# Putting off the second half of the softmax, giving the fourth output block and two rows of x a buffer of their own, and loading the branch rows two at a time, in a two-layer diffusion step

## The chip, the cores and the metric

One program runs on one core of a Trainium2 chip. The metric is the device time of one execution in microseconds (us). A core has five engines with an instruction stream each, executed in order: PE (TensorE, matrix products into PSUM), DVE (VectorE), ACT (ScalarE), POOL (GpSimd) and SP (SyncE, which here only issues transfers). They wait for one another through semaphores. Transfers run on 16 DMA engines that all issuers share.

## The reference, cut to what matters

Two layers work on 1280 tokens of 1024 channels: 256 context tokens (`x_prompt`) and 1024 latent tokens (`x_sample`). Layer 0 mixes tokens with a gated linear scan (GLA, 4 heads, forwards and backwards), layer 1 with softmax attention (8 heads of 128, 2 key heads; a latent query sees 1024 latent and 256 cached keys, a context query 256 context keys). Each layer normalises and modulates its input, projects it, mixes, multiplies by a SiLU gate, projects with `w_out`, and adds the result times a per-channel gate `gt` to `x`.

```
hs = rms_norm(xs, norm_g[l]) * (1.0 + sc_s) + sh_s
y  = (mixer(hs @ w_in) * silu(gate)) @ w_out
xs = xs + gt_s * y
p  = softmax(q @ keys.T * scale);  o = p @ vals        # layer 1
```

The outputs are both streams after layer 1, the scan states, and the new keys and values.

## The kernel before

Every matrix operand is held as two float16 parts, hi and lo, and every product is three matmuls (hi·hi, hi·lo, lo·hi) that accumulate in float32. So a row or a weight block must be scaled, split into hi and lo, and, where it is the contracted side, transposed by a DMA before PE can use it. Tokens come in tiles of 128 rows; tiles 0 and 1 are context, 2 to 9 latent. The transposed, modulated activations of all tokens stay on chip in `hT_hi` and `hT_lo`. Weight blocks live in three kept places (`wtile(0)`, `wtile(1)`, `wtile(2)`), each with a hi and a lo half of 512 columns; `wst` is a small ring of staging buffers, `wada` another one for the modulation weights.

The program runs in stages. A list scheduler in the language orders each engine's instructions from the order in which the code issues them; `issue_after(x)` gives code the place right behind instruction x.

- **Load and modulation, then the GLA loop** (`gla`, from about 140 us). Five passes h over ten tiles n; slot = 10h + n. In each slot a tile's scan and gate work is interleaved with fillers from the function `filler(slot)`: modulation weights, weights of layer 1 split ahead of time, and from slot 32 the output projection of layer 0. At the slots in `WO` (32, 36, 38, 40) a quarter of `w_out` (256 columns) is staged, and `fill_out` scales and splits it (DVE L161, L175; ACT L174): the first two into place 0, the third into the place that the last gate block used, the fourth into place 2. At slot 43 `fold_gate` loads the gate row `gt_d` and multiplies it by the four blocks' inverse scales on POOL (L712, eight instructions). At the slots in `PREP` (42, 44, 46) a finished branch row `og_d[i]` (128 tokens, 512 KB) is loaded, measured (DVE L745), split (ACT L748, DVE L749) and transposed (SP L751, L752); at those in `EARLY` (45, 47) tiles 2 and 3 get their `residual` (output projection, times gate, plus x) and are stored to `x1_d`.
- **gla_out** (about 582 to 782 us). For the ten tiles in the order 2 to 9, 0, 1: `residual` (PE L125 into the banks y; DVE L723 times gate, L724 plus x), and per pair of tiles `normalise` (ACT L329, DVE L332), PE transposes (L337) and `modulate` (ACT L348, POOL L349, DVE L350), then `key_tile`, which projects keys and values, normalises and rotates the keys and transposes them. Tiles 2 and 3 are read back from `x1_d`. `out_load` loads the next branch row into `og`, which has one buffer; `out_prep` is as above, with one DMA transpose of 2048 columns into `ogT` (SP L754).
- **attention** (about 782 to 1258 us). Ten steps (a half of the heads, a block of 256 queries) of four heads e. `scores(h, c, j, ...)` does one softmax tile of 128 queries by 1280 keys: nine matmuls into S (PE L974), the row maximum (DVE L977), its scaling (ACT L979), the exponential p with its row sum (ACT L982), the reciprocal (DVE L984, L986), the hi part of p divided (POOL L989), the lo part (DVE L990) and one DMA transpose into PT (SP L991). S has two buffers in PSUM, p and the pair phl two, PT three, one for each head. `values` (30 matmuls with PT, then DVE L1015) is two heads behind; `query`/`query_rest` (24 matmuls of 512 columns and the work on ACT, DVE and POOL) prepare the queries of a later step; two `gateT` (24 matmuls each) stand at the end of every second head.
- **att_out** (from about 1258 us): the output projection of layer 1, row by row, stored to the output.

For a pair of heads (plain and with a prime) the code before writes S0, query, S1, V, S0', S1', V', G, G; on PE the scheduler puts the first 11 of the 30 matmuls of V' ahead of S1'.

## Time and profile before

| | |
|---|---|
| median of three runs | 1352.31 us (1348.84 to 1357.2) |
| the profiled execution | 1360.72 us |
| its span in the trace | 1358.9 us |
| mean granted PE clock | 0.978 |
| PE busy | 1245.7 us, 92% |
| DVE, ACT, POOL busy | 69%, 49%, 28% |
| moved by DMA | 199.14 MB, mean 147 GB/s |

The profile is of one execution, somewhat slower than the median. A busy time of PE of 92% is a mean over stages: the idle time sits in particular places, and the waits table of a window says how often and for how long an engine stood idle, and which instruction of which engine ended the wait. A wait is written "waiter <- releaser". The windows table gives for each stretch the length, then busy us of each engine, the granted PE clock, the share of time that the DMA engines were busy, and GB/s.

### The profile page before, as it was taken

Reading aid. Unit: us, or ns where it says so; the run is one execution under the profiler, and the core shown is the slowest. Engines: PE = TensorE matmul, PEld = TensorE weight load, DVE = VectorE, ACT = ScalarE, POOL = GpSimd, SP = SyncE. Lnnn points to the kernel's source line nnn. Section 1 sums busy time; section 2 is a strip of 40 time slices with the busy share of each in tenths; the row PEclk is TensorE's granted clock in tenths of the full one; section 3 lists DMA queues with packets and bytes.
Section 4 is the critical chain, followed back from the end, with each engine's and each line's share of the span. In section 5 each row is a group of like instructions: output and inputs, shape, how many; then the busy total and the mean of one; then the engine's idle time right before and its main releaser. Section 6 shows DMA issues by size and latency. Waiting matters only on the chain. (4 is left out here: it accounts for less than half of the span.)

```text
span 1358.9 us, 22664 instructions
## 1 busy us (share of the span) xinstructions
PE 1245.7 (92%) x8150; PEld 808.9 (60%) x8150; DVE 931.1 (69%) x2138; ACT 669.7 (49%) x1661; POOL 382.8 (28%) x623
## 2 busy tenths in 40 slices
PE   4789999999999999697889989899999989989998
PEld 2357765655555556475657656666676756665444
DVE  1776868886867788755654567777768677875552
ACT  2565646655646567523323455555566555562110
POOL 1232212422322133401222534333233343422000
PEclk9899999999999999898989999999999989999999
DMA  9612455544545532377543268576859638887532
GB/s 306 219 62 95 140 178 182 168 154 133 187 132 178 160 113 78 101 214 198 129 127 121 60 181 155 104 137 121 188 102 188 128 83 145 182 156 171 174 132 78
DMA packets 344769, 199.14 MB, mean 147 GB/s; under 512 B 229406, under 2 KB 331534, under 8 KB 343376
## 3 DMA queue, kind: packets, MB, share of 16 engines
q1 hardware_dynamic: 297024, 159.67, 47.3%
q10 hardware_dynamic: 47312, 37.25, 8.5%
q8 instruction: 64, 1.05, 0.3%
q0 software_dynamic: 320, 0.77, 0.2%
q14 instruction: 49, 0.40, 0.1%
HBM read 104.31 MB, written 37.24 MB: 104 GB/s over the span
## 5 line engine op out<-in xcount | busy, mean ns | idle before, releaser
L125 PE MATMUL mm<-whi,hT_hi 128*128 128x512 f16 (+1 forms) x560 | 197.1, 352 | 12.1 <-ACT gx L471 7.4
L125 PEld LDWEIGHTS <-hT_hi 128*128 128x128 f16 x1440 | 142.2, 99 | 109.9 <-issue 15.4
L125 PE MATMUL mm<-wlo,hT_hi 128*128 128x512 f16 (+1 forms) x560 | 196.8, 351 | 0.0
L125 PE MATMUL mm<-whi,hT_lo 128*128 128x512 f16 (+1 forms) x560 | 196.6, 351 | 0.0
L125 PEld LDWEIGHTS <-whi 128*128 128x128 f16 x1368 | 135.5, 99 | 90.5 <-issue 21.7
L125 PE MATMUL mm<-hT_hi,whi 128*128 128x256 f16 (+1 forms) x512 | 155.2, 305 | 10.5 <-DVE og L1015 5.4
L989 POOL TENSOR_SCALAR phl<-p,srec 128x1280 f16<-128x1280 f32 (+1 forms) x80 | 99.9, 1250 | 218.7 <-DVE srec L984 146.2
L125 PE MATMUL mm<-hT_lo,whi 128*128 128x256 f16 (+1 forms) x512 | 155.5, 304 | 0.2 <-DVE hT_lo L350 0.2
L125 PE MATMUL mm<-hT_hi,wlo 128*128 128x256 f16 (+1 forms) x512 | 155.4, 304 | 0.0
L990 DVE SCALAR_TENSOR_TENSOR phl<-p,srec,phl 128x1280 f16<-128x1280 f32 (+1 forms) x80 | 107.5, 1344 | 59.0 <-POOL phl L989 58.9
L974 PE MATMUL S<-kT,wst 128*128 128x512 f16 (+1 forms) x624 | 122.9, 338 | 14.4 <-ACT p L982 14.4
L125 PE MATMUL mm<-PT,vh 128*128 128x256 f16 x672 | 113.7, 273 | 4.9 <-DMA PT<-phl 4.5
L977 DVE TENSOR_REDUCE smx<-S 128x1 f32<-128x1280 f32 (+1 forms) x80 | 101.0, 1267 | 3.3 <-PE S L974 3.3
L982 ACT ACTIVATE p<-S,snb,sexp 128x1280 f32<-128x1280 f32 (+1 forms) x80 | 99.3, 1241 | 5.0 <-DVE srec L984 1.1
L125 PEld LDWEIGHTS <-hT_lo 128*128 128x128 f16 x720 | 71.1, 99 | 49.7 <-issue 1.0
L974 PEld LDWEIGHTS <-wst 128*128 128x128 f16 x624 | 61.0, 98 | 65.8 <-issue 16.2
L125 PEld LDWEIGHTS <-wlo 128*128 128x128 f16 x720 | 71.3, 99 | 39.6 <-issue 2.8
L125 PE MATMUL mm<-PT,vl 128*128 128x256 f16 x336 | 91.6, 273 | 0.0
L125 PE MATMUL y<-whi,ogT 128*128 128x256 f16 (+1 forms) x336 | 76.6, 318 | 6.7 <-DVE xr L724 4.6
L147 DVE TENSOR_REDUCE wmx<-wst 128x1 f32<-128x512 f32 x104 | 64.5, 676 | 26.5 <-DMA wst<-in_gla_w_in 10.7
L979 ACT ACTIVATE snb<-smx,nsexp 128x1 f32<-128x1 f32 x80 | 23.4, 292 | 115.7 <-DVE smx L977 115.7
L125 PEld LDWEIGHTS <-vh 128*128 128x128 f16 x672 | 65.4, 98 | 15.0 <-issue 4.3
(335 smaller groups left out, 2696.8 us busy)
## 6 DMA issues: line engine op xcount, KB each, us to landing
wada<-in_w_ada SPq DMA_DIRECT2D x16, 1024.0 KB, 5.0
wst<-in_gla_w_in SPq DMA_DIRECT2D x12, 1024.0 KB, 5.8
wst<-in_att_w_in SPq DMA_DIRECT2D x10, 1024.0 KB, 8.3
xr<-x_d SPq DMA_DIRECT2D x11, 512.0 KB, 3.3
og_d<-gx ACTq DMA_DIRECT2D x40, 128.0 KB, 1.8
og_d<-og ACTq DMA_DIRECT2D x40, 128.0 KB, 3.8
wst<-og_d SPq DMA_DIRECT2D x5, 1024.0 KB
out<-xr ACTq DMA_DIRECT2D x17, 256.0 KB, 2.0
```

The costliest lines, as they stand in the source:

```text
L125: self.nc.tensor.matmul(out, a, b, start=k == 0 and j == 0, stop=k == n - 1 and j == 2)
L147: nc.vector.tensor_reduce(mx[:, j : j + 1], st[:, 2 * j : 2 * j + 2, :], AX.XY, ALU.max, apply_absolute_value=True)
L974: nc.tensor.matmul(S[:, a : a + n], x, y, start=m == 0, stop=m == 2)
L977: nc.vector.tensor_reduce(mx, S, AX.X, ALU.max)
L979: nc.scalar.activation(nb, mx, AF.Copy, scale=self.nsexp)
L982: nc.scalar.activation(p, S, AF.Exp, scale=self.sexp, bias=nb, accum_out=den)
L989: nc.gpsimd.tensor_scalar(hi, p, r, 2.0 ** 14, ALU.mult, ALU.mult)
L990: nc.vector.scalar_tensor_tensor(lo, p, r2, hi, ALU.mult, ALU.subtract)
```

## The change

It has four parts.

1. **GLA tail.** `WO` becomes (30, 32, 36, 38), so each of the four blocks of `w_out` is filled two slots earlier. The fourth goes into a `wada` buffer of the pool `ada`, which now stays open to the end of `gla_out`, and not into place 2. Place 2 then takes, at slot 40, the x rows of tiles 2 and 3 (in its hi half) and two of the four parts of the key and value weights `w_kv` (in its lo half). `fold_gate` is cut into the load (`gate_load`, at slot 40) and the multiplication, a job run after slot 40 (POOL L717). A fourth row is prepared early (`PREP` has 48 too). The early residuals work in place on the x rows on chip, and a job after slot 47 normalises the pair. Two small GLA weights (`wa1`, `wa2`) are staged in a `wada` buffer.
2. **gla_out.** The loop starts at tile 4, with tiles 2 and 3 already normalised; they are not read back. `og` and `oghl` have two buffers, and two loads of rows are issued at the start. Every branch row is transposed straight into its own columns of `hT_hi` and `hT_lo` (two DMA transposes of 1024 columns, SP L753 and L754), which the modulation overwrites later; `ogT` is gone. `att_setup` and `key_setup` are issued behind the last modulation of the first pair.
3. **Softmax's second half put off.** What `scores` did from the reciprocal on is now the method `rest`, kept in `put_off`, and run by the next call of `scores` behind that tile's row maximum. So the reciprocal, POOL's hi part, the lo part and the transpose of one tile come behind the maximum of the next tile.
4. **Order in a pair of heads.** The code writes S0, query, S1, V, S0', V', S1', G, G. The load of the first output row (`out2_load`) is issued one head earlier than its preparation.

The core of the diff:

```
-WO = (32, 36, 38, 40)
-PREP = (42, 44, 46)
+WO = (30, 32, 36, 38)
+PREP = (42, 44, 46, 48)
...
-            og = self.t(self.xp, [P, D], F32, "og", bufs=1)
-            parts = self.t(self.xp, [P, 2 * D], F16, "oghl", bufs=1)
-            to = self.t(self.xp, [P, 2 * KT, P], F16, "ogT", bufs=3)
+            og = self.t(self.xp, [P, D], F32, "og", bufs=2)
+            t = self.t(self.xp, [P, 2 * D], F16, "oghl", bufs=2)
+            parts = t[:, 0:D], t[:, D:]
...
+        to = [t[:, :, i * P : i * P + P] for t in (self.hT_hi, self.hT_lo)]
+        nc.sync.dma_start_transpose(to[0], hi)
+        nc.sync.dma_start_transpose(to[1], lo)
...
-            nc.sync.dma_start(x, self.x1_d[i] if n < len(EARLY) else xrow(self.I, i))
+            nc.sync.dma_start(x, xrow(self.I, i))
...
-        nc.vector.tensor_reduce(mx, S, AX.X, ALU.max)
+        last = nc.vector.tensor_reduce(mx, S, AX.X, ALU.max).ins
...
         nc.scalar.activation(p, S, AF.Exp, scale=self.sexp, bias=nb, accum_out=den)
+        self.rest(last)
+        self.last = last
+        self.put_off = p, den, PT, j, nk
...
                 if e % 2 == 0:
                     self.query()
+                    self.scores(h, c, 1, q[(p, c, 1)], PT)
                 else:
                     self.query_rest()
-                self.scores(h, c, 1, q[(p, c, 1)], PT)
                 if len(pend) == 2:
                     self.values(*pend[0], g.pop(pend.pop(0)[0]))
+                if e % 2 == 1:
+                    self.scores(h, c, 1, q[(p, c, 1)], PT)
...
+            if slot == 40:
+                k.jobs.append((k.fold_gate, *k.gate_load(0), [t[2] for t in wo]))
                 wo[:] = [(*k.w0[0:2], 512)] + [(hi, lo, 256) for hi, lo, _ in wo[2:]]
+                k.w2 = k.wtile(2)
+                t = k.w2[0].rearrange("p k n -> p (k n)").bitcast(F32)
+                for n in range(2):
+                    xs.append(t[:, D * n : D * n + D])
+                    load(xs[n], xrow(I, NTP + n))
```

How this moves instructions shows at three places. The first is DVE in a steady pair of heads, from the softmax tile S0 to the next one, S1 (before, then after). `smx` is a row maximum, `srec` the reciprocal, `phl` the lo part, `hrsa` and `hx` are the normalisation of the queries.

```order
L984 RECIPROCAL srec_11233<-sden_11231 128x1
L986 TENSOR_SCALAR srec_2586_11235<-srec_11233 128x1
L990 SCALAR_TENSOR_TENSOR phl_11237<-p_11230,srec_2586_11235,phl_11237 128x1280
L114 TENSOR_SCALAR hrsa_11273<-hssq_11269 128x2
L977 TENSOR_REDUCE smx_11293<-S_11283 128x1
L114 TENSOR_SCALAR hrsa_11372<-hssq_11368 128x2
```

```order
L114 TENSOR_SCALAR hrsa_11265<-hssq_11261 128x2
L979 TENSOR_REDUCE smx_11285<-S_11275 128x1
L1000 RECIPROCAL srec_11292<-sden_11223 128x1
L114 TENSOR_SCALAR hrsa_11364<-hssq_11360 128x2
L826 SCALAR_TENSOR_TENSOR hx_2580_11233<-hx_2580_11233,hrs_11267,qn_7384 128x128 x2
L1002 TENSOR_SCALAR srec_2593_11294<-srec_11292 128x1
L1006 SCALAR_TENSOR_TENSOR phl_11296<-p_11222,srec_2593_11294,phl_11296 128x1280
```

The lo part of S0 stood ahead of the maximum of S1 and now stands behind it.

The second is SP in `gla_out`, at the loads of branch rows `og` (before, then after).

```order
L754 DMA_TRANSPOSE ogT_7379<-oghl_7378 128x16x128
L739 DMA og_7406<-og_d_64 128x1024
L853 DMA_TRANSPOSE kT_7577<-xhl_7594 128x4x128
L853 DMA_TRANSPOSE kT_7577<-xhl_7598 128x4x128
L772 DMA xr_8031<-in_x_sample 128x1024
L754 DMA_TRANSPOSE ogT_7408<-oghl_7407 128x16x128
L739 DMA og_7617<-og_d_64 128x1024
```

```order
L741 DMA og_7379<-og_d_64 128x1024
L741 DMA og_7405<-og_d_64 128x1024
L774 DMA xr_7408<-in_x_sample 128x1024
L774 DMA xr_7619<-in_x_sample 128x1024
L774 DMA xr_7875<-in_x_sample 128x1024
L774 DMA xr_8029<-in_x_sample 128x1024
L860 DMA ropet_7382<-in_k_rope 128x2048
L862 DMA qn_7384<-in_att_qnorm 128x128
L864 DMA kn_7386<-in_att_knorm 128x128
L753 DMA_TRANSPOSE hT_hi_71<-oghl_7380 128x8x128
L754 DMA_TRANSPOSE hT_lo_72<-oghl_7380 128x8x128
L741 DMA og_7616<-og_d_64 128x1024
```

A load of a row stood behind the transposition of the row before it; now two loads lead, and the third stands behind the transposition of the first.

The third is POOL around slot 40, where the gate is folded (before, then after). `Sa` and `Sc` are scan states, `at` the inner products of a chunk, `ors` a reciprocal root, `wst` with `p2i` the gate row and a block's inverse scale.

```order
L116 TENSOR_TENSOR ors_6744<-orsa_6742,mhalf_81 128x1
L116 TENSOR_TENSOR ors_6798<-orsa_6796,mhalf_81 128x1
L571 TENSOR_SCALAR Sc_7302<-Wc_7257,eb_1419_5438,eb_1378_5296 128x256
L116 TENSOR_TENSOR ors_6874<-orsa_6872,mhalf_81 128x1
L712 TENSOR_SCALAR wst_6816<-wst_6816,p2i_5810 128x256
L712 TENSOR_SCALAR wst_6816<-wst_6816,p2i_6295 128x256
```

```order
L538 TENSOR_TENSOR at_6289<-am_26_142 128x128
L717 TENSOR_SCALAR wst_6644<-wst_6644,p2i_5541 128x256
L717 TENSOR_SCALAR wst_6644<-wst_6644,p2i_5841 128x256
L717 TENSOR_SCALAR wst_6644<-wst_6644,p2i_6326 128x256
L717 TENSOR_SCALAR wst_6644<-wst_6644,p2i_5541 128x256
L717 TENSOR_SCALAR wst_6644<-wst_6644,p2i_5841 128x256
L717 TENSOR_SCALAR wst_6644<-wst_6644,p2i_6326 128x256
L572 TENSOR_SCALAR Sa_6583<-Wa_6467,eb_1712_6391,eb_1740_6485 128x256
L116 TENSOR_TENSOR ors_6453<-orsa_6451,mhalf_81 128x1
L538 TENSOR_TENSOR at_6438<-am_25_141 128x128
```

Six of the eight multiplications of the gate moved from behind the last inner products to ahead of a scan state and an `at` of the last scan tiles.

159 lines of the change are left out of this document (84 added, 75 removed).

## The prediction

> **What bounds the kernel now.** I read the page first, then the windows by stage, then who waited for what on PE in each, then timelines at the dear places.
>
> ```profile
> PE 1245.7 (92%) x8150; PEld 808.9 (60%) x8150; DVE 931.1 (69%) x2138; ACT 669.7 (49%) x1661; POOL 382.8 (28%) x623
> 544.00:582.00 38.00, 27.64 (x168) 19.57 (x169) 26.63 (x77) 20.19 (x56) 14.57 (x25) 0.87 0.37 98
> 582.00:612.00 30.00, 30.00 (x230) 22.30 (x228) 15.57 (x29) 8.04 (x18) 0.00 (x0) 1.00 0.80 239
> 612.00:782.00 170.00, 151.57 (x1104) 110.61 (x1102) 94.53 (x239) 61.37 (x150) 47.63 (x105) 0.95 0.46 127
> 782.00:830.00 48.00, 41.49 (x272) 26.76 (x270) 32.59 (x61) 27.00 (x71) 19.62 (x25) 0.96 0.72 170
> 830.00:1000.00 170.00, 158.83 (x1135) 110.73 (x1134) 127.71 (x228) 93.98 (x236) 60.73 (x82) 1.00 0.74 139
> 1000.00:1150.00 150.00, 144.60 (x1002) 98.96 (x1000) 113.06 (x253) 91.55 (x257) 56.77 (x88) 0.98 0.68 131
> 1150.00:1250.00 100.00, 91.92 (x675) 65.64 (x674) 73.54 (x124) 52.11 (x113) 33.59 (x44) 1.00 0.85 174
> ```
>
> PE is the bound; the change removes almost no matmul, so it can only win PE's idle time and its slow clock. Length less PE busy gives the idle time of the stages touched: 10.4 us in the GLA tail, 18.4 in gla_out, 6.5 + 11.2 + 5.4 + 8.1 = 31.2 in attention. The clock costs at most 0.13·38 + 0.05·170 + 0.04·48 + 0.02·150, some 18 us. That is the ceiling: near 78 us.
>
> **Attention.** PE's waits from 782 to 1250 us, and one of them from close by:
>
> ```profile
> PE S L974 <- ACT p L982: 14.4, 10, 2.1
> PE mm L125 <- DVE og L1015: 5.4, 5, 3.6
> PE mm L125 <- DMA PT<-phl: 4.5, 4, 2.2
> 840.32 1.79 PE L974 MATMUL S<-kT,wst 128*128 128x512 f16 x9
> 841.63 1.33 POOL L989 TENSOR_SCALAR phl<-p,srec 128x1280 f16<-128x1280 f32 x1 [3.46 <-DMA PT<-phl]
> 843.00 1.55 DVE L990 SCALAR_TENSOR_TENSOR phl<-p,srec,phl 128x1280 f16<-128x1280 f32 x1 [2.33 <-POOL phl L989]
> 845.21 1.78 PE L974 MATMUL S<-kT,wst 128*128 128x512 f16 x9
> 846.84 0.38 PE L125 MATMUL mm<-PT,vh 128*128 128x256 f16 x2
> 846.89 1.49 DVE L977 TENSOR_REDUCE smx<-S 128x1 f32<-128x1280 f32 x1
> 848.79 1.42 ACT L982 ACTIVATE p<-S,snb,sexp 128x1280 f32<-128x1280 f32 x1
> 850.35 1.78 PE L974 MATMUL S<-kT,wst 128*128 128x512 f16 x9 [2.15 <-ACT p L982]
> 854.04 0.27 PE L125 MATMUL mm<-hT_hi,whi 128*128 128x256 f16 x1
> 856.66 1.24 PE L974 MATMUL S<-kT,wst 128*128 128x512 f16 x5
> ```
>
> S1 runs at 840.32, its maximum only at 846.89: DVE does the lo part of the tile before first, which waits for POOL, which waits for an older transposition to free phl. The exponential ends at 850.2 and PE, which needs that one of the two S buffers for S1', has stood 2.15 us. Between 854.04 and 856.66 lie the 24 matmuls of a G: 2.62 us, 0.109 each. So V (30) is 3.27; S is 846.84 − 845.21 = 1.63; its six wide matmuls are 0.217 each, a query (24) 5.2.
>
> The change acts twice here. The maximum no longer stands behind the second half of the tile before (a query's norm, L114, still stands ahead of it); and from the end of S1 to S1' lie now V, S0' and V', 8.2 us, for 3.27 + 1.63 + 11·0.109 = 6.1. Maximum and exponential take about 3.5 us from when DVE is free, so the ten waits of 14.4 us should go; of the 5.4 for og (a bank freed late by DVE) I take 1 to 2. The waits for PT (4.5) are kept, and those that the table has besides. Bounds: nothing below, 14.4 + 5.4 = 20 above.
>
> What it costs is time on the way to PT. After S1' comes G, G and the next S0, 6.9 us, then that tile's maximum, and only then the second half of S1'.
>
> ```profile
> DMA to landing us min/median/max: 2.5/5.1/7.5
> L989 POOL TENSOR_SCALAR phl<-p,srec x26: 478/1334/1576, 841.6 to 997.1; 128x1280 f16<-128x1280 f32 x24, 128x256 f16<-128x256 f32 x2
> DMA to landing us min/median/max: 2.4/5.3/9.4
> ```
>
> The first row is the landing of the 27 transposes of 840 to 1000 us, the second POOL's hi part there, the last the landing over all 80. The chain: 6.9 + 1.5 (maximum) + 0.4 (reciprocal, start of POOL) + 1.3 + 1.6 (lo) + 0.2 + 5.1 = 17.0 us. The V' that reads S1' comes behind G, G, S0, query, S1, V, S0' of the next pair: 5.2 + 1.6 + 5.2 + 1.6 + 3.3 + 1.6 = 18.5. Before, 19 matmuls of V' more lay between, and the second half began at once. So 1.5 us of slack: free at the median, 0.9 us late at a landing of 7.5, 2.8 at 9.4. I charge a third of 18 pairs with 0.5: 3 us, from 0 to 18·2.8 = 50. The other tiles have more: their successor follows after 4.9 us at most, or they are read later. Net for attention: 14.4 + 1.6 − 3 = **13 us won**.
>
> Here the Trainium skill speaks against the change: "SBUF — State Buffer", section "SBUF: two separate sides", says that DVE operations with two SBUF inputs and GpSimd operations exclude each other from a shared port pair for a whole instruction. POOL's hi part of S1' now falls among DVE's silu of the two G. The row of the hi part (1334 ns median, 1576 at most) shows 0.24 us of such a delay; by the rule a whole DVE operation, an estimated 1.55 us if it is as long as the lo part, would use up the slack, and the charge would be 10 us or more in place of 3.
>
> **gla_out.** PE's waits, DVE's, and the loop behind them:
>
> ```profile
> PE tr L337 <- DVE xr L332: 4.6, 1, 4.6
> PE y L125 <- DVE xr L724: 4.6, 1, 4.6
> PE tr L337 <- ACT h L348: 3.7, 1, 3.7
> PE kv L84 <- DVE amx L874: 1.5, 1, 1.5
> DVE wm L745 <- DMA og<-og_d: 19.8, 6, 6.5
> 661.62 1.85 SPq L754 DMA_TRANSPOSE ogT<-oghl  x1
> 663.56 1.05 SPq L739 DMA_DIRECT2D og<-og_d  x1
> 669.82 1.22 DVE L745 TENSOR_REDUCE wm<-og 128x1 f32<-128x1024 f32 x1 [6.47 <-DMA og<-og_d]
> 680.00:714.00 34.00, 29.36 (x201) 20.22 (x200) 18.10 (x41) 10.13 (x24) 8.09 (x17) 0.90 0.43 124
> ```
>
> With one buffer the load of a row waits for the transposition of the last one (661.62), then takes 6.3 us, and DVE, in order, stands 6.47 us at its maximum; all that PE needs of DVE (L724 frees y) is queued behind. With two buffers the load starts a row earlier, and some 15 us of PE work pass per row (151.57 busy for ten rows), twice the landing. So y (4.6) and h (3.7) go: 8.3 us. The first pair is already normalised, so the 4.6 at L332 goes too, though tile 4 now leads and its x lands behind two rows; I take half, 2.3. amx moves behind the modulation: 1. The clock of 0.90 in 680 to 714 costs up to 3.4; half of it comes back, 1.7. Against: one more transpose issue per row (1.85 us for one of 2048 columns stands on SP, which is not full) and the two loads of x that land with the rows: −1.5. Sum: **12 us won**, from 5 (loads late all the same) to 20.
>
> **GLA tail.**
>
> ```profile
> PE mm L125 <- ACT gx L471: 6.5, 2, 6.0
> 561.89 1.41 DVE L175 SCALAR_TENSOR_TENSOR wlo<-wst,wso,whi 128x512 f16<-128x512 f32 x2
> 569.22 0.47 ACT L471 ACTIVATE gx<-mm,inv_g 128x256 f32<-128x256 f32 x1 [2.39 <-DMA og_d<-gx]
> L712 POOL TENSOR_SCALAR wst<-wst,p2i x8: 474/480/482, 567.6 to 570.8; 128x256 f32<-128x256 f32 x8
> 534.08 0.56 POOL L571 TENSOR_SCALAR Sa<-Wa,eb,eb 128x256 f32<-128x256 f32 x1 [1.29 <-PE A L591]
> 524.81 0.38 PE L125 MATMUL mm<-whi,hT_lo 128*128 128x512 f16 x1
> ```
>
> The long wait here is a gate behind ACT's queue, late because DVE splits the fourth block (561.89) in between. That block comes two slots earlier: 2.5 to 5 us less DVE in the way; of the 6.0 I take 4, from 0 to 8. But six multiplications of the gate now stand on POOL ahead of a scan state. They need the gate row, and on SP that load stands behind four transfers (2 MB) that wait until place 2 is free, near 524.8. Three MB at the 239 GB/s of 582 to 612 land at 538, six times 0.48 end at 541; the scan state ran at 534.08. If so POOL is 6.6 us late, and `at`, which PE's scan needs, behind it. Some of it replaces the wait later. Cost 2 to 3, from 0 to 7. Net: **1.5 us won**, from −7 to +8. Of the earlier fills one more lies between slots 30 and 33; I charge 1 for DVE's share of it.
>
> **att_out.** DVE waits for its first row at the end of attention:
>
> ```profile
> DVE wmx L1090 <- DMA wst<-og_d: 6.1, 2, 3.4
> ```
>
> That load is now issued a head earlier; DVE is on PE's way there only in part: 1.5 of the 3.4, from 0. Moving the small GLA weights costs nothing, since the start waits for x and weights.
>
> **Sum.** 13 + 12 + 1.5 − 1 + 1.5 = 27 us of the profiled 1360.7, so 1333.7; that execution stands 8.4 us above the median of 1352.3, a difference that I keep, so I forecast a median of **1325 us**.
>
> **Rivals.**
> (A) *PT takes the place of S.* The putting-off makes V' wait one to two us in most pairs. For: 1.5 us of slack against a landing between 2.4 and 9.4. Against: two transposes that came 1.6 us apart now come 4.9 apart. With 18 pairs times 0.9 = 16 in place of 3 the gain in attention is gone: 27 − 13 = 14, 1338 us.
> (B) *The row loads stay late.* Two rows and four tiles of x in a row on one queue land in 10 us and more, and DVE still stands at L745. For: xr and og share the DMA. Against: 0.43 share in 680 to 714. gla_out then wins 5: 20 in all, 1332 us.
> (C) *Slower.* V' waits in every pair for PT because transposes land late beside weight loads (DMA share 0.85 in 1150 to 1250): at a landing of 9.4 us, 18·2.8 = 50 lost for 30 won elsewhere (27 with the 3 taken back): 1352 + 20 = 1372 us. It decides against the change from a mean landing of 6.6 + 30/18 = 8.3 us. Against it: the medians 5.1 and 5.3. The Trainium skill's "DMA: Bandwidth & Descriptors", section "Issuing engines are not separate DMA queues", says that all DMAs run on the same 16 engines and interleave, which would feed this case.
> (D) *The gate on POOL* stalls the scan by the full 7 us and nothing of the gate wait goes: 27 − 8.5 = 18.5, 1334 us.
>
> **How the numbers follow.** Forecast 0.55 (own range 1312 to 1336), A 0.2, B 0.1, D 0.07, C 0.08. Over 1% (13.5 us, about what a measurement can tell from no change) faster means under 1338.8: all of the forecast but a twentieth, rather more than half of A, most of B and D: 0.78. Within 1%: the rest of these, 0.15. Slower: C for the most part, 0.07. The range reaches to A and a part of what lies under it: 1300 (52 of the 78 us at the ceiling) to 1345.
>
> **What would show it.** Right: S <- p gone from PE's waits; wm <- og below 5 us; no idle time of 4 us at transposes or y in gla_out; PT waits under 5 us in all. Wrong: mm <- PT of over 15 us (A, C); wm <- og still near 20 (B); a wait of PE for A or o of over 4 us near slot 40 with POOL in L717 behind a DMA (D). A shorter span with S <- p still there would make the reason wrong though the time be right.

## The result, and the profile after

The changed kernel takes 1336.91 us (median of 4 runs, 1334.62 to 1340.19). The kernel before took 1351.6 us beside it (4 runs, 1348.84 to 1357.2). The ratio is 0.9877, with a 95% interval of 0.9847 to 0.9906; the medians give 14.7 us, this ratio some 17. The profiled execution took 1338.16 us, 22.5 less than that of before. The forecast was 1325 us.

PE is still the bound, with 8 us less busy time and 22.5 us less span. The matmul records are as many as before (8150), so these 8 us are the same matmuls run in less time; the mean granted clock is 0.982 after 0.978. The row is that of the changed kernel's page.

```profile
PE 1237.8 (93%) x8150; PEld 808.0 (60%) x8150; DVE 929.4 (70%) x2138; ACT 661.4 (49%) x1661; POOL 403.1 (30%) x623
```

Next the windows of the changed kernel. The columns are the stretch in us, its length, the busy time of PE, PEld, DVE, ACT and POOL, PE's granted clock, the DMA share and GB/s.

```profile
582.00:612.00 30.00, 28.56 (x215) 20.89 (x214) 15.54 (x31) 10.13 (x21) 0.70 (x1) 1.00 0.72 201
612.00:782.00 170.00, 159.93 (x1189) 117.38 (x1189) 99.93 (x250) 68.32 (x176) 48.25 (x108) 0.98 0.49 142
782.00:816.00 34.00, 27.59 (x180) 18.34 (x179) 28.61 (x48) 16.96 (x41) 17.56 (x26) 0.90 0.66 116
816.00:952.00 136.00, 135.78 (x969) 94.39 (x967) 106.85 (x191) 78.89 (x201) 61.44 (x67) 1.00 0.78 142
952.00:1122.00 170.00, 157.26 (x1117) 110.28 (x1114) 120.90 (x274) 97.19 (x277) 64.75 (x98) 0.98 0.68 131
1122.00:1215.00 93.00, 86.02 (x628) 61.97 (x626) 72.64 (x122) 49.80 (x116) 38.02 (x41) 0.98 0.83 163
```

Length less PE busy again gives the idle time. gla_out has 1.4 + 10.1 us where it had 18.4. The attention, now 767 to 1215 us, splits sharply: 0.2 us in 136 of the steady steps, but 6.4 in its first 34, 12.7 between 952 and 1122 and 7.0 at the end.

What PE waited for in the changed kernel, first in 582 to 782 us, then in 765 to 1250:

```profile
PE y L125 <- DVE xr L729: 6.3, 1, 6.3
PE S L976 <- ACT p L984: 2.0, 1, 2.0
PE kv L125 <- DVE hT_lo L350: 1.7, 2, 1.4
```

```profile
PE mm L125 <- DMA PT<-phl: 19.1, 8, 6.4
PE mm L125 <- ACT snb L981: 3.3, 1, 3.3
PE S L976 <- ACT p L984: 2.9, 2, 2.0
PE mm L125 <- issue: 2.4, 1, 2.4
```

Of the three long waits of gla_out (4.6, 4.6, 3.7) two are gone, and one of 6.3 us stands at the start of the stage. In the attention the waits for the exponential fell from 14.4 to 2.9 us, and those for PT rose from 4.5 to 19.1.

Two profiled executions can differ by several us for no reason that lies in the change. So three marks on PE's timeline cut each profile into stages: the first matmul into y, the first into S, the end of the span. They are the first starts of these rows (before, then after; the row gives count, min/median/max in ns, first and last start):

```profile
L125 PE MATMUL y<-whi,wlo x48: 272/273/379, 602.3 to 612.7; 128*128 128x256 f16 x32, 128*128 128x512 f16 x16
L974 PE MATMUL S<-kT,wst x624: 272/379/379, 784.8 to 1227.8; 128*128 128x512 f16 x96, 128*128 128x256 f16 x60
```

```profile
L125 PE MATMUL y<-whi,hT_hi x128: 272/326/631, 599.5 to 728.5; 128*128 128x512 f16 x64, 128*128 128x256 f16 x64
L976 PE MATMUL S<-kT,wst x624: 272/379/379, 767.5 to 1210.7; 128*128 128x512 f16 x96, 128*128 128x256 f16 x60
```

From first to last score before took 443.0 us and after 443.2. By these two rows the attention's loop, on which 13 of the 27 us rested, gained nothing. They are a rough measure, since in the new order the last score tile stands behind all of its V' and less work follows it. From the first score to the end of the span before took 574.1 us and after 568.9. The experiments ask why so little came, and where the gain came from.

### The profile page after: what moved, and what is told of

Read it like the earlier page. It is cut to its first block, busy times and chain, and to the rows that moved or that the text cites. A ratio compares the mean times of both kernels' runs of the same rounds, so it can differ in the third digit from the quotient of the medians.

```text
span 1336.4 us, 22681 instructions
## 1 busy us (share of the span) xinstructions
PE 1237.8 (93%) x8150; PEld 808.0 (60%) x8150; DVE 929.4 (70%) x2138; ACT 661.4 (49%) x1661; POOL 403.1 (30%) x623
## 5 line engine op out<-in xcount | busy, mean ns | idle before, releaser
L125 PEld LDWEIGHTS <-hT_hi 128*128 128x128 f16 x1920 | 188.1, 98 | 128.1 <-issue 12.8
L125 PEld LDWEIGHTS <-whi 128*128 128x128 f16 x1296 | 128.0, 99 | 72.5 <-issue 10.0
L1005 POOL TENSOR_SCALAR phl<-p,srec 128x1280 f16<-128x1280 f32 (+1 forms) x80 | 105.9, 1324 | 204.7 <-DVE srec L1000 110.3
L125 PE MATMUL mm<-PT,vh 128*128 128x256 f16 x672 | 118.0, 281 | 24.9 <-DMA PT<-phl 19.1
L125 PEld LDWEIGHTS <-hT_lo 128*128 128x128 f16 x960 | 94.0, 98 | 62.6 <-DVE hT_lo L350 2.7
L984 ACT ACTIVATE p<-S,snb,sexp 128x1280 f32<-128x1280 f32 (+1 forms) x80 | 99.6, 1244 | 16.9 <-DVE srec L1000 7.6
L125 PE MATMUL mm<-PT,vl 128*128 128x256 f16 x336 | 94.5, 281 | 0.0
L147 DVE TENSOR_REDUCE wmx<-wst 128x1 f32<-128x512 f32 x104 | 64.6, 677 | 29.2 <-DMA wst<-in_gla_w_in 11.5
L125 PEld LDWEIGHTS <-wlo 128*128 128x128 f16 x648 | 63.9, 99 | 34.3 <-issue 1.9
L837 POOL TENSOR_TENSOR rope<-hx,ropet 128x64 f32<-128x64 f32 x160 | 66.1, 442 | 15.2 <-DVE hx L826 7.1
```

Source lines behind the costliest of these rows:

```text
L125: self.nc.tensor.matmul(out, a, b, start=k == 0 and j == 0, stop=k == n - 1 and j == 2)
L147: nc.vector.tensor_reduce(mx[:, j : j + 1], st[:, 2 * j : 2 * j + 2, :], AX.XY, ALU.max, apply_absolute_value=True)
L837: nc.gpsimd.tensor_tensor(tv[:, h, :, w, :], xv[:, h, :, 1 - w, :], sn[:, :, w, :], ALU.mult)
L984: nc.scalar.activation(p, S, AF.Exp, scale=self.sexp, bias=nb, accum_out=den)
L1005: nc.gpsimd.tensor_scalar(hi, p, r, 2.0 ** 14, ALU.mult, ALU.mult)
```

## The experiments

All marks in one table: for each kernel the median, the ratio to the kernel before on the same chip, and from its profile the time to the first y, from there to the first S, and from there to the end of the span.

| kernel | us | ratio (95%) | to y | y to S | S to end |
|---|---|---|---|---|---|
| before | 1351.6 | | 602.3 | 182.5 | 574.1 |
| before_again | 1357.07 | 1.0009 (0.9979–1.0039) | 603.5 | 176.9 | 573.8 |
| after | 1336.91 | 0.9877 (0.9847–0.9906) | 599.5 | 167.9 | 568.9 |
| att_old | 1339.42 | 0.9872 (0.9848–0.9896) | 602.0 | 170.8 | 564.5 |
| order_only | 1338.55 | 0.9868 (0.9844–0.9892) | 600.8 | 170.4 | 565.6 |
| putoff_only | 1349.28 | 0.993 (0.9901–0.996) | 599.8 | 174.0 | 577.3 |
| last_prompt | 1335.81 | 0.9847 (0.9814–0.988) | 599.7 | 170.1 | 566.0 |
| og1 | 1337.18 | 0.9869 (0.9838–0.99) | 596.8 | 170.9 | 564.7 |
| three_prep | 1333.99 | 0.985 (0.9818–0.9882) | 598.4 | 167.3 | 563.2 |
| gate_late | 1337.85 | 0.9867 (0.9836–0.9898) | 600.0 | 170.1 | 565.7 |
| rows_first | 1339.45 | 0.9875 (0.9839–0.9912) | 605.7 | 168.4 | 566.3 |
| reload_x | 1338.2 | 0.9875 (0.9845–0.9905) | 599.5 | 174.5 | 561.9 |
| best | 1325.69 | 0.9785 (0.9756–0.9815) | 597.7 | 168.9 | 558.2 |
| before_two | 1348.23 | 0.9947 (0.9913–0.9982) | 608.3 | 176.5 | 563.5 |

The intervals are some 0.3% to each side, so only steps of about 8 us stand apart in the ratio. A smaller one can be seen only as a wait that comes or goes in the profile.

### The attention: two halves, together and apart

The first four runs asked where the attention's 13 us went. **att_old**: the changed kernel with the softmax finished at once and the old order.

```
-        self.rest(last)
...
         self.put_off = p, den, PT, j, nk
+        self.rest()
...
                 if e % 2 == 0:
                     self.query()
-                    self.scores(h, c, 1, q[(p, c, 1)], PT)
                 else:
                     self.query_rest()
+                self.scores(h, c, 1, q[(p, c, 1)], PT)
...
-                if e % 2 == 1:
-                    self.scores(h, c, 1, q[(p, c, 1)], PT)
```

> The changed kernel with its attention as it was before (softmax finished at once, both score tiles of a head ahead of the values). Theory 1 (the putting-off trades PE's waits for p against waits for PT, one for one): attention lasts 443 us as in both traces, the time is that of the changed kernel, 1337 us, within 4; S <- p near 14 us again, mm <- PT near 4. Rival 2 (attention got faster in most executions, the profiled one hides it): 8 to 12 us slower than the changed kernel.

Measured: 1339.42 us, 0.9872; the changed kernel had 0.9877. PE's waits in its attention, 767 to 1215 us (the 19.1 us of the changed kernel all lie in that stretch too):

```profile
PE S L976 <- ACT p L984: 13.1, 11, 2.6
PE mm L125 <- DMA PT<-phl: 6.7, 4, 3.8
PE mm L125 <- DVE og L1031: 1.8, 4, 0.7
```

The S waits are back, most of the PT waits are gone (a fifth, of 3.6 us, stands behind the stretch, at 1227), and the time is the same, as Theory 1 said. Its 443 us between first and last score did not come: 432.6, with more work behind the last score. Putting off and the new order together are worth nothing that can be measured here.

**order_only** keeps the new order and finishes the softmax at once (the first of the two hunks above); **putoff_only** keeps the putting-off with the old order (the second).

> The changed kernel with each softmax finished at once; the new order of scores and values stays. Theory 1: the wait S <- p falls under 6 us because 8.2 us lie between the tiles, and mm <- PT falls back under 8: 8 to 14 us faster than the changed kernel, near 1326. Rival 2 (DVE's and POOL's order sets the pace, not the distance on PE): S <- p stays at 10 us or more and the time within 4 us of 1337.

> The changed kernel with the old order (both score tiles ahead of the values) and the putting-off. Theory 1: the row maximum is early, so S <- p is under 8 us; a tile has 2 us more until its values, so mm <- PT is 8 to 14 us: 3 to 8 us faster than the changed kernel. Rival 2: mm <- PT near 19 as in the changed kernel, S <- p 5 to 10 more: 5 us slower.

order_only, 0.9868, waits 9.5 us for PT, 7.4 for og and 5.4 for S between 765 and 1250 us: S fell as its Theory 1 said, the time is its rival's. putoff_only, 0.993, waits 18.5 for PT, as its rival said, and S stays under 8, as its Theory 1 said; but by the medians it is slower than either said. From first S to the end it takes 577.3 us, 12.8 more than att_old (6.3 of it idle time of PE, 6.5 busy time of the same matmuls at a lower clock), and its median is 9.9 us above att_old's. So putting off costs some 10 us in the old order and is free in the new one; neither half wins against the old attention.

**last_prompt** finishes the last tile of each pair of heads, the one with 1.5 us of slack in the prediction, at once:

```
                 if e % 2 == 1:
                     self.scores(h, c, 1, q[(p, c, 1)], PT)
+                    self.rest()
```

> The changed kernel, but the second half of the last tile of a pair of heads is not put off (rest is called right after it). Theory 1 with the slack of the prediction (that tile alone is late): mm <- PT from 19 to under 8 us, S <- p unchanged near 3: 8 to 12 us faster, near 1327. Rival 3 (the PT waits are of other tiles: at the start, where DVE is behind, and at the short context blocks): mm <- PT stays over 12 us and the time within 4 us of 1337.

Measured: 0.9847, 566.0 us from first S to the end, and 18.7 us of PT waits (19.1 in the changed kernel). The total, the time and the places are the rival's. But the edit did not act where most of the waits stand. DVE takes the reciprocal of S1' ahead of the next tile's maximum in 16 of 19 pairs; in the other three, at the start and behind the two context blocks, the scheduler leaves it behind that maximum, and these three hold 11.4 of the 18.7 us. Where it did act, three V' wait 6.9 us in all, after 5.3 in the changed kernel, so there the putting-off of that tile is not what costs. But the run can't show that another tile is late: the trace says that it is S1'.

Where the waits stand, the windows above say already: at the start and from 952 us on, not in the steady steps. One of them in the changed kernel, with its rows on POOL, DVE, SP and PE in this order. Each row is start, us, engine, line and operation; the bracket is the idle time before it and what ended it.

```profile
1102.04 1.58 POOL L1005 TENSOR_SCALAR phl<-p,srec 128x1280 f16<-128x1280 f32 x1 [4.55 <-DMA PT<-phl]
```

```profile
1098.41 1.54 DVE L1006 SCALAR_TENSOR_TENSOR phl<-p,srec,phl 128x1280 f16<-128x1280 f32 x1
1099.87 1.48 DVE L979 TENSOR_REDUCE smx<-S 128x1 f32<-128x1280 f32 x1
1101.27 0.15 DVE L1000 RECIPROCAL srec<-sden 128x1 f32<-128x1 f32 x1
1103.65 1.55 DVE L1006 SCALAR_TENSOR_TENSOR phl<-p,srec,phl 128x1280 f16<-128x1280 f32 x1 [1.17 <-POOL phl L1005]
```

```profile
1104.56 1.22 SPq L855 DMA_TRANSPOSE wst<-xhl  x1
1105.87 8.21 SPq L1007 DMA_TRANSPOSE PT<-phl  x2
```

```profile
1089.35 1.79 PE L976 MATMUL S<-kT,wst 128*128 128x512 f16 x9
1105.29 1.78 PE L976 MATMUL S<-kT,wst 128*128 128x512 f16 x9
1111.29 0.41 PE L125 MATMUL mm<-PT,vh 128*128 128x256 f16 x2 [4.22 <-DMA PT<-phl]
```

Counting the softmax tiles, their 80 transpositions and PE's V in order tells which tile a wait is for. The V' at 1111.29 needs the S1' that ran at 1089.35. Only one G followed it, so the next tile was done 4.2 us after S1', not 6.9. But DVE still had the lo part of an earlier tile to do (1098.41), and took that next tile's maximum only at 1099.87; the reciprocal of S1' stands behind it, at 1101.27. POOL then waits until 1102.04 for an older transposition to free phl (0.6 us; the rest of its 4.55 us of idle time lies before the reciprocal). The lo part follows, SP passes a query's transposition first, the issue is at 1105.87, and the landing lets V' start. From the end of S1' that is 20 us, where the prediction worked out 17.0. PE's other work ended at 1107.07, 15.9 us after S1', where it worked out 18.5. In the steady pairs the same count gives 16.7 to 18.7 us against 18.4.

This wait stands just behind the second context block, where a softmax tile is three matmuls in place of nine and a V six in place of thirty. By this count seven of the eight waits, 16.9 of the 19.1 us, are a V' that waits for S1': 6.4 at the start, 6.5 behind the context blocks, 3.8 in the last two steps and 0.2 in the steady ones.

### gla_out and the tail, part by part

**og1**: one row buffer again.

```
-            og = self.t(self.xp, [P, D], F32, "og", bufs=2)
-            t = self.t(self.xp, [P, 2 * D], F16, "oghl", bufs=2)
+            og = self.t(self.xp, [P, D], F32, "og", bufs=1)
+            t = self.t(self.xp, [P, 2 * D], F16, "oghl", bufs=1)
```

> The changed kernel with one row buffer (og and oghl once each) in place of two in the output projection of the GLA block; everything else as changed. Theory 1 (the second row buffer is what took the stalls at about 669 and 695 us out of that stage): wm<-og on VectorE goes from 13.0 us back to about 20, PE waits of 3 to 5 us at the residual (y<-xr) and at the transposes (tr<-h) come back, sum 6 to 9 us; the stall y<-xr of 6.3 us at 611 falls to 3 to 5, since only one row's maximum then stands ahead of the first residual; time 4 to 7 us above the changed kernel's 1336.9, that is 1341 to 1344, ratio to the kernel before 0.990 to 0.993. Rival (the stalls went because the branch rows are transposed into hT and the setup of the keys stands later, the buffer adds nothing): no stall of over 2 us at 640 to 700, 1335 to 1338.

Measured: 0.9869. The longest wait of its gla_out:

```profile
PE y L125 <- DVE p2e L94: 8.5, 2, 4.8
```

One of the two stands at the start of the stage and is 1.5 us shorter than the 6.3 of the changed kernel; the other, 3.7 us, is back late in the stage, at 682. Theory 1 is wrong in its size: the second buffer takes off some 4 us late in the stage and adds a part of it at the start, and DVE's wait for rows, 11.9 us, did not go back to 20. The time, 1337.18 us, is the rival's, though its "no stall of over 2 us" is not met.

**three_prep**: three early rows in place of four.

```
-PREP = (42, 44, 46, 48)
+PREP = (42, 44, 46)
...
-        rows = {len(early): self.out_load(order[len(early)])}
+        prep[order[3]] = self.out_prep(*self.out_load(order[3]))
+        rows = {4: self.out_load(order[4])}
...
-            if n + 3 < NT and n + 3 >= len(early):
+            if n + 3 < NT and n + 3 >= 5:
```

> The changed kernel with three branch rows prepared in the GLA tail in place of four; the fourth is loaded and prepared at the start of the output projection, and the fifth is loaded behind it. Theory 1 (the fourth early row gives the first load of the stage the time that it needs): PE reaches the fourth row's tile about 21 us after the stage begins at 604 (two tiles of 10.6 us), its row lands at 613 and its transposes at about 624 as the fifth row's did, so it waits 3 to 8 us and later rows are later by as much; 4 to 8 us above the changed kernel, 1341 to 1345. Rival (two tiles are cover enough): wait under 2 us, 1335 to 1339.

Measured: 0.985, and 167.3 us from y to S. The longest wait of the stage is 3.0 us, at a transpose. By the time the rival holds: the fourth early row gives nothing that can be measured, and two tiles of PE work are cover enough.

**gate_late**: the gate's multiplications queued behind the last `at`.

```
-        nc.gpsimd.tensor_tensor(at, am[:, 0, :], am[:, 1, :], ALU.add)
+        self.at_ins = nc.gpsimd.tensor_tensor(at, am[:, 0, :], am[:, 1, :], ALU.add).ins
...
-    def fold_gate(self, gt, inv):
+    def fold_gate(self, gt, inv, after=None):
+        if after is not None:
+            with self.tc.issue_after(after):
+                return self.fold_gate(gt, inv)
...
-                k.jobs.append((k.fold_gate, *k.gate_load(0), [t[2] for t in wo]))
+                k.jobs.append((k.fold_gate, *k.gate_load(0), [t[2] for t in wo], k.at_ins))
```

> The changed kernel with the eight multiplications of the gate row queued on GpSimd behind the last sum at of the intra part, so that GpSimd doesn't stand at the gate row's load at 537 to 539 us ahead of Sa and at. Theory 1 (GpSimd's place for the gate is what PE waits for in the tail): PE's waits A<-POOL at (2.7 us in 535 to 582) go to under 1, U<-POOL Sc (2.4) to about 1; 2 to 4 us below the changed kernel, 1333 to 1335; ratio about 0.985. Rival (the tail's chain of decayed states decides, and the wait moves to the next sum): sum of the tail's waits unchanged within 1 us, 1336 to 1338.

In the changed kernel POOL stands for the gate row's load as predicted:

```profile
539.36 3.61 POOL L717 TENSOR_SCALAR wst<-wst,p2i 128x256 f32<-128x256 f32 x6 [2.32 <-DMA wst<-gt_d]
```

PE's waits between 535 and 582 us, in the changed kernel and in gate_late:

```profile
PE A L592 <- POOL at L538: 2.7, 2, 1.5
PE U L604 <- POOL Sc L572: 2.4, 1, 2.4
PE mm L125 <- ACT gx L472: 1.2, 1, 1.2
```

```profile
PE cs L604 <- POOL Sc L572: 1.4, 1, 1.4
PE U L604 <- POOL Sc L572: 1.4, 1, 1.4
PE o L604 <- POOL Sc L572: 1.4, 2, 0.7
PE A L592 <- POOL at L538: 1.2, 1, 1.2
```

With three of 0.2 to 0.5 us that aren't shown the sum falls from 7.2 to 5.4 us, and 4.2 of it stand at the states Sc now, where 3.1 stood. First y is at 600.0 in place of 599.5, the ratio 0.9867. The waits moved nearly as Theory 1 said, the time as the rival said: the gate's place on POOL isn't what decides the tail.

**rows_first**: cache loads and half of `w_kv` queued behind the first row load.

```
-        self.nc.sync.dma_start(og, self.og_d[i])
+        self.row_ins = self.nc.sync.dma_start(og, self.og_d[i]).ins
...
-        ckv = self.att_load()
+        with self.tc.issue_after(self.row_ins):
+            ckv = self.att_load()
...
+                    if j == 0:
+                        with self.tc.issue_after(self.row_ins):
+                            nc.sync.dma_start(hi, d[:, 0, :, b])
+                            nc.sync.dma_start(lo, d[:, 1, :, b])
```

> The changed kernel with the loads of cache_k, cache_v and one half of w_kv queued on SP behind the first row load of the output projection (1 MB of w_kv behind the second row and the first x row). Theory 1 (the stall y<-xr of 6.3 us at 611 is the two row loads issued at 605 and 607 behind these): the first row is issued at 601 and lands at about 608, the residual L729 runs 3 to 4 us earlier, the stall falls to 2 to 3 us; 3 to 4 us below the changed kernel, 1333 to 1334. Rival (the x row lands as late, since the bytes of the stage are the limit there): the stall stays at 5 to 7 us, 1335 to 1338.

The wait y<-xr falls from 6.3 to 1.0 us, but 3.4 at transposes and 2.5 for hT come in its place, and y to S is 168.4 us, as in the changed kernel. The window of the changed kernel in which the long wait lies shows why:

```profile
604.00:618.00 14.00, 7.70 (x60) 5.83 (x58) 8.52 (x24) 2.79 (x6) 0.08 (x1) 0.83 1.06 366
```

A DMA share of 1.06 at 366 GB/s: the DMA engines are busy throughout, so moving one load forward moves another back. The rival holds in its reason, though the wait went to other rows and did not stay. The time, 1339.45 us, is above both. The profiled execution reached y late, at 605.7, with nothing edited ahead of it, so its whole length isn't to be read.

**reload_x**: the two x rows read back from memory and normalised in gla_out, as before the change.

```
-                if n == 1:
-                    k.jobs.append((k.normalise, xs, k.t(k.qkp, [P, 512], F32, "q0").bitcast(F16)))
...
-        done, xs = (order[0], first), []
+        done, xs = None, []
...
-        for n in range(len(first), NT):
+        for n in range(NT):
...
-            nc.sync.dma_start(x, xrow(self.I, i))
-            self.residual(i, lambda k: (hT[:, k, :], lT[:, k, :]), wo, inv, x)
-            nc.scalar.dma_start(self.x1_d[i], x)
+            nc.sync.dma_start(x, self.x1_d[i] if n < len(first) else xrow(self.I, i))
+            if n >= len(first):
+                self.residual(i, lambda k: (hT[:, k, :], lT[:, k, :]), wo, inv, x)
+                nc.scalar.dma_start(self.x1_d[i], x)
```

> The changed kernel without the two x rows kept on chip: both are loaded again from the stored x1 at the start of the output projection and normalised there, as before the change; the rest as changed. Theory 1 (the kept rows, normalised in the tail, are the largest part of what the output projection gained, since one row buffer in place of two and three early rows in place of four cost nothing measurable): the wait tr<-xr L332 of 4 to 5 us stands at the stage's first transposes again, later stages of the chain run behind by as much; first residual to first score 173 to 178 us in place of 167 to 171; 3 to 7 us above the changed kernel, 1340 to 1344. Rival (the stage's first loads decide anyway: a stall of 5 to 6 us stands there in the changed kernel too): 167 to 171, 1335 to 1338.

Its waits in gla_out begin with

```profile
PE y L125 <- DVE xr L729: 13.2, 2, 12.8
```

and y to S takes 174.5 us, within Theory 1's 173 to 178. But the wait stands at the residual and not at the transposes where it was expected, and the same wait is 6.1 to 10.0 us in kernels whose stage is unedited (att_old 6.1, putoff_only 10.0, with 174.0 us from y to S). The time, 0.9875, is the rival's. So what the kept rows are worth is at most a few us, and this run doesn't set it apart from the scatter.

### The attention again

**before_again**: the kernel before, profiled once more, without an edit.

> The kernel before, unchanged, profiled once more, because its profiled execution (1360.7 us) was the longest of its runs and the difference of the two profiles (22.5 us) is larger than that of the medians (14.7). Marks on PE in the first profile: first residual of the output projection at 602.3 us, first score 784.8, last score 1227.8. Theory 1 (the gain is the tail's and the output projection's, the attention gave none): the stage from first residual to first score takes 180 to 183 us again (changed kernel and its variants so far 167 to 174), and from the first score to the end about 562 in place of 570, as the kernel with the old attention in the new frame had (560 to 562). Rival (the old attention is slower by itself): 568 to 571 again. Time 1349 to 1358.

First S to end: 573.8 us, after 574.1 the first time. The expectation counts to the start of PE's last matmul: there it is 569.8 after 570.0. So Theory 1's 562 was wrong and the rival's 568 to 571 came. But att_old, with the same softmax and the same order, takes 564.5 to the end of the span. Something in the change that is neither the putting-off nor the order wins 9 us in the attention: 3.8 of idle time of PE and 5.5 of its busy time, over the same 3540 matmuls, at a clock of 0.99 after 0.98. In the stretch from 765 to 1215 us two waits of before_again are not in att_old (of the first, its longest), which has 6.2 us more for PT there:

```profile
PE mm L125 <- DVE og L1015: 5.7, 5, 3.9
PE mm L125 <- ACT rope L930: 3.7, 1, 3.7
```

The first is one wait of 3.90 us at 1087.46, and DVE's timeline shows what stands ahead of og:

```profile
1084.27 2.35 DVE L1090 TENSOR_REDUCE wmx<-wst 128x1 f32<-128x1024 f32 x2 [3.58 <-DMA wst<-og_d]
1086.53 0.41 DVE L235 TENSOR_TENSOR gx<-gx,ls 128x256 f32<-128x256 f32 x1
1086.86 0.15 DVE L1094 TENSOR_TENSOR wm<-wmx 128x1 f32<-128x1 f32 x1
1086.93 0.47 DVE L1015 SCALAR_TENSOR_TENSOR og<-mm,inv_o,gx 128x256 f32<-128x256 f32 x1
```

That is the preparation of att_out's first row. The code has it in the last step, but the scheduler put it some 100 us earlier on DVE, where it stands 3.58 us for the row's load, with og and the bank that PE needs behind it. The change issues the load one head earlier and binds the preparation behind the last step's maximum: L1090's successor L1114 first runs at 1185.1 us. The second wait stands ahead of the first query of the attention, whose bank of PSUM ACT still holds with the last value tile:

```profile
785.42 0.47 ACT L930 ACTIVATE rope<-kv,inv_av 128x256 f32<-128x256 f32 x1 [2.55 <-DMA out<-rope]
```

In att_old ACT still stands 3.11 us for that DMA, but PE doesn't wait for it: the change takes the four held banks in another order, a line that the core of the diff above doesn't show. **before_two** is the kernel before with these two things alone:

```
-            k.held = {t: k.bank(t) for t in ("y", "tr", "mm", "kv")}
+            k.held = {t: k.bank(t) for t in ("y", "tr", "kv", "mm")}
...
-        nc.vector.tensor_reduce(mx, S, AX.X, ALU.max)
+        self.last = nc.vector.tensor_reduce(mx, S, AX.X, ALU.max).ins
...
+                if n == 9 and e == 0:
+                    row = self.out2_load(OUT[0])
...
-                    self.prep = self.out2_prep(OUT[0], (first[:, 0], first[:, 1]))
+                    with self.tc.issue_after(self.last):
+                        self.prep = self.out2_prep(row, (first[:, 0], first[:, 1]))
```

> The kernel before with two small parts of the change alone: the banks of PSUM held over the key stage are taken in the order y, tr, kv, mm in place of y, tr, mm, kv, and the first output row of the attention is loaded at the last step and prepared behind that step's last row maximum, where before its preparation stood at 1084 us on VectorE, 3.6 us for the row's load, ahead of og. Old softmax, old order, old GLA tail and output projection. Theory (these two, not the putting-off and the new order, are what the attention part of the change won, since the kernel with the old attention in the new frame had 560 us from first score to end and the kernel before 570 twice): PE's waits mm<-rope (4.8 and 3.7) and mm<-og at 1083 to 1088 (3.8 and 4.1) are gone, from first score to end 561 to 564 us; 6 to 9 us below the kernel before, ratio 0.993 to 0.996. Rival (the 10 us come from the new frame, where the attention starts with other transfers under way): 568 to 570, ratio 0.998 to 1.001.

Measured: 1348.23 us, ratio 0.9947 (0.9913 to 0.9982), 7.8 us by the medians. First S to end is 563.5 us; the wait for rope is gone, and og has 1.6 us in 3 waits. So the theory holds, in the waits and in the time: these two edits bring as much as the attention's part of the change. Of the 10 us from first S to the end, 2.7 are idle time against the second profile of the kernel before and 5.9 against the first; the rest is busy time of the same matmuls, at a clock of 1.00 after 0.98 and 0.99. Whether the two waits lowered that clock wasn't tested, and neither was each edit alone.

**best** puts together what the runs suggest: three early rows, the gate behind `at`, and the old attention only at and beside the two context blocks, where the PT waits stand.

```
+            self.prompt = 0 in [c for _, c in self.steps[max(n - 1, 0) : n + 2]]
...
         self.put_off = p, den, PT, j, nk
+        if self.prompt:
+            self.rest()
...
                     self.query_rest()
+                    if self.prompt:
+                        self.scores(h, c, 1, q[(p, c, 1)], PT)
...
-                if e % 2 == 1:
+                if e % 2 == 1 and not self.prompt:
                     self.scores(h, c, 1, q[(p, c, 1)], PT)
```

> The changed kernel with three early rows (as in the run three_prep), the gate's multiplications behind the last at (as in gate_late), and in the attention the softmax finished at once and the old order of scores and values in steps 3 to 7 of the ten, that is at and beside the two short context blocks; put off as in the changed kernel in steps 0 to 2, 8 and 9. Theory 1 (the PT stalls of putting off stand at the context blocks and cost about 12 us between 952 and 1120 us, where the old order loses 5): PE's waits mm<-PT go from 19 to 25 us to 10 or 12, S<-p rises by at most 3; with the 2 to 3 us of the early rows 1326 to 1331, ratio 0.979 to 0.982. Rival (the sum of the attention's waits stays at 21 to 28 us whatever the order, as in the four variants so far): 1333 to 1337, ratio 0.985 to 0.987.

Measured: 1325.69 us (1323.51 to 1331.57), ratio 0.9785 (0.9756 to 0.9815), below both kernels and apart from the changed one's interval. The stretch that held 12.7 us of PE idle time in the changed kernel, in best:

```profile
940.00:1112.00 172.00, 166.76 (x1202) 117.17 (x1201) 131.85 (x295) 107.57 (x303) 65.66 (x101) 1.00 0.73 143
```

172 less 166.76 is 5.2 us of idle time, 7.5 less. Of the 12.7 us the PT waits were 6.5, and 3.8 are left; a wait of 3.3 us for ACT (snb) and one of 2.4 with no releaser in the profile are gone. Over the whole attention the PT waits are 16.0 us where 10 to 12 were expected: those at the start and in the last steps stay. The early rows and the gate are in the same kernel; their share of the gain was not taken apart, and the interval of three_prep alone begins just where that of best ends (0.9818 and 0.9815).

## Why the prediction was right and wrong

The direction was right and the time lies in the range, though just above the forecast's own 1312 to 1336; 27 us were forecast and 14.7 came by the medians. By its own list of signs most reasons were not borne out: wm<-og is 13.0 us where under 5 was named, a wait of 6.3 us stands at y where none of 4 was to, and PT is 19.1 where under 5 was named and over 15 was to speak for rival A. A's time, 1338 us, is within 1.1 us of the result. That is luck in part: A had the waits in most pairs and the attention's gain gone; they stand in a few pairs, and the attention gained 8.9 us by another way.

- **Attention, 13 us.** From first S to the end the six profiles with the changed attention as it is (after, og1, three_prep, gate_late, rows_first, reload_x) take 565.1 us on average, and the two of the kernel before 574.0: 8.9 us. But none of it came by the named way: att_old, without that way, takes 564.5. The step that failed is "I charge a third of 18 pairs with 0.5: 3 us": the S waits did fall, by 11.5 us, and PT rose by 14.6. The tile was the right one, and both terms, 17.0 and 18.5, were right for the steady pairs (16.7 to 18.7 and 18.4; 0.2 us of idle time in 136). But they were taken over to all 18. At the start and behind the context blocks the work that covers is 14.7 to 15.9 us, and at the two longest waits the chain is 20 to 21, because DVE comes late to the next tile's maximum; the sum had no term for that.
- **"And those that the table has besides" are kept.** This hid much of the gain. The wait for rope (4.6 us in the first profile) stood in that table and went; of og "1 to 2" were taken, and a single wait of 3.6 went.
- **att_out, 1.5 us.** The load that is late was seen (6.1 us, longest 3.4), but placed at the end of the attention. A look at the start of the row, 1089 us in the first profile, would have shown it in the middle, ahead of og.
- **gla_out, 12 us.** y to S takes 170.6 us on average in the six profiles with this stage unedited (after, att_old, order_only, putoff_only, last_prompt, gate_late), and 178.6 in the three of the old stage: 8 us. The term for the second buffer (8.3) was too large, by og1; a new wait of 6.3 us stands where 2.3 were taken off, because the stage's first loads fill the queues. One of the two waits in the 8.3, of 4.6 us at y, isn't in the second profile of the kernel before at all. What the kept rows, for which 2.3 was taken, are worth, reload_x leaves open. The wait at the transposes at 669 us and the setup of the keys put behind weren't tried alone. So where the 8 us come from is shown only in part.
- **GLA tail, 1.5 − 1.** The gate row landed at 539.4 where 538 was worked out, and POOL was done at 543.0 where 541 was. PE's long wait for gx fell from 6.0 to 1.2, and 2.7 for `at` came: the net was of the right order (the second of the four fills moved by four slots, not by two), though first y varies from 596.8 to 605.7 among kernels that share this part, so no finer statement holds.
- **The clock, 1.7 us.** Against the first profile of the kernel before the span lost 22.5 us, 7.9 of them busy time of PE; against the second 17.8, and 12.9 of them. It is the same 8150 matmuls each time, at a mean clock of 0.978 and 0.974 before and 0.982 after. So between a third and three quarters of the difference of the profiles is no idle time at all, and the sum had 1.7 us for it. Slow matmuls follow a wait: behind the 4.22 us at 1111.29 two matmuls of V' take 0.63 us that took 0.38 before it, at a granted clock of 0.54 from 1111.29 to 1114 us after 1.00 from 1100 to 1107. So a wait that goes can win more than its length, but no run shows how much of the clock hangs on the waits: the mean clock is 0.973 to 0.982 over 52 executions of the kernel before, and 0.980 to 0.982 in the four of the changed one.
- **The sum** was made against an execution 8.4 us above its median, and this difference was kept. It should not have been: the second profile of the kernel before, at 1356.0 us, has 5.6 us less from y to S with the same code. A long wait in one profile is partly that execution's.
- **The Trainium skill's** "SBUF — State Buffer", "SBUF: two separate sides", was weighed against POOL's hi part. Over all 80 hi parts, before and after the change:

```profile
L989 POOL TENSOR_SCALAR phl<-p,srec x80: 475/1334/2101, 796.7 to 1240.0; 128x1280 f16<-128x1280 f32 x64, 128x256 f16<-128x256 f32 x16
L1005 POOL TENSOR_SCALAR phl<-p,srec x80: 471/1395/2807, 781.3 to 1222.6; 128x1280 f16<-128x1280 f32 x64, 128x256 f16<-128x256 f32 x16
```

The median rose from 1334 to 1395 ns and the longest from 2101 to 2807. (The 1576 of the prediction is the longest of 26 between 840 and 1000 us only; delays of up to 0.8 us were there before.) The longest began at 1017.22, 0.2 us after a lo part on DVE (1017.04, 1.53 us), and ended 1.46 us after that lo part did, about one undisturbed hi part. That agrees with the rule; no run shows that the port is its cause, or what it adds to the PT waits.

## What to carry to other kernels

Slack worked out in the steady part of a loop says nothing about its ends and its short iterations: there the cover is thin and the other engines are behind, and a longer chain costs what it saves elsewhere; the old order beside the short blocks, together with two small edits, brought 0.9% more. Before a wait is put down to a shortage, look for what stands ahead of it in its engine's queue: a preparation that came too early and the order of four banks brought as much as the attention's whole part of the change. After an edit that is to move an instruction, look on the trace whether it moved: where most of the waits stood, last_prompt moved nothing. And profile the kernel before twice, before a sum is built on one execution's waits.

## What the runs showed of the hardware

- The median landing of the attention's transpositions did not change, though their issues come a little further apart (5.6 us in the median, 5.0 before):

```profile
DMA to landing us min/median/max: 2.4/5.3/8.1
```

  Before, these were 2.4, 5.3 and 9.4. The traces hold a landing for 26 and 21 of the 80 transpositions, so these are no figures of all 80. POOL, whose next hi part writes where the transposition reads, stood 40.3 us in 11 cases for a landing in the changed kernel, and 56.7 us in 17 cases before.
- Two kernels that differ only in gla_out, og1 and rows_first, reached its first y 8.9 us apart (596.8 and 605.7 us). Of this 6.8 us are busy time of PE over the same 3420 matmuls (544.4 and 551.2 us), at a mean clock of 0.983 and 0.977 up to there. So most of such a difference between two executions is in how fast the same matmuls ran; what set that isn't shown.
